# A hybrid encoder layer in split fp32: operand combinations dealt out between gated-unit tiles, mixed tiles loaded into the scan's copy pages, and two casts of the feed-forward asked for one piece later

## The chip, the core and the metric

The kernel runs on one core of a Trainium2 chip. The time is the device time of one execution in microseconds (us); the time of a kernel is the median of its runs. Engines are named as the profile does: PE is TensorE (PEld its weight loads), DVE VectorE, ACT ScalarE, POOL GpSimd, SP SyncE, whose queue issues nearly all DMAs.

## What is computed

One encoder layer over x of 1024 positions and 1024 channels, all in float32:

```
h    = rmsnorm(x)
proj = h @ w_in                                  # 1024 x 8192, cut into 8 parts
glu_in, q, v, z_f, z_b, og, g_a, g_b = split(proj)
a    = glu(glu_in)                               # 512 channels
a    = silu(layernorm(dwconv31(a))) @ conv_pw_w  # mixer A
o    = hgrn2 scan over q, v, z_f + the same backwards over z_b   # 8 heads of 128
b    = (rmsnorm per head(o) * silu(og)) @ hgrn_o_w               # mixer B
x    = x + (sigmoid(g_a) * a + sigmoid(g_b) * b) @ w_out
h2   = rmsnorm(x)
gate, val = split(h2 @ ffn_w_up)
x    = x + (silu(dwconv3(gate)) * val) @ ffn_w_down
out  = rmsnorm(x)
```

## The kernel before

**Products in split fp32.** A float32 operand is kept as two tiles, a rounded part and a rest: `split` (L124) makes the first with a cast on ScalarE and the second with a subtraction on VectorE. A product of two such operands is three matmuls (L148 to L150) into one PSUM bank. Weights come as `wr` pages (512 KB, two of them) through SyncE's queue (L135) and are split into `wp` pages; activations lie in `hx` and `hy` pages of 128 x 512.

**Seven products for eight.** Most of the large products use Strassen's scheme: seven products of half-size blocks, each with a sum or difference of blocks on either side. The activations' sums are made by `combos` (L457 on): it takes three blocks `b11`, `b12`, `b22`, makes b12 - b22 into a `tm` page, and from that two further blocks in place, each split at once (rows L465 and L124 with `hy`). The function `h_combos` (L936 on) does this for the four values of k: it loads three blocks from the DRAM copy `d_h` into `su` pages (four of them) and calls `combos`. The weights' sums are made by a generator (around L414) that hands control back with `yield n`: its next step comes n pieces of matmul later.

**Streams.** Matmul work is cut into pieces. A `Stream` holds generators of such pieces, and `fill(n)` writes n of them into the program where it is called, so that TensorE's work stands between the other engines' work. The order of the text is then the order in which the pieces are handed to a scheduler at build time, which orders each engine's queue; an instruction waits for its operands and for its page to come free, and every queue is in order.

**The first place, 75 to 125 us.** The gated unit's tiles (`s_glu`) are projections whose banks are read by a sigmoid on ScalarE (L850) and a multiplication on VectorE (L856). They are followed by the 31-tap convolution on VectorE (L1035, L1038, into `acc`), which runs through the whole convolution stage beside the pair jobs on TensorE up to about 345 us; the pair jobs' banks are read by VectorE at L799. Before, all four calls of `combos` are handed over first and then 17 pieces of the gated unit:

```
    h_combos()
    s_glu.fill(GLU_LATE)
```

**The second place, 825 to 905 us.** The scan over 16 half-heads alternates with dense work. It copies `qF` and `kG` into `A` pages (L1175, eight of them), turns `kG` on TensorE (L1320) and copies it to `kT` (L1322), for the state products of L1329. Each head's mixed output (`bm`) goes to DRAM, but for the last head. Behind the scan, `bm_loads` brings the seven others back, half by half, for the product with `hgrn_o_w` (mixer B): `load` (L117) takes one of four `tm` pages, and the tile is split into `hx` pages.

Of the kernel before, what the change touches and what calls it, by code (L numbers as in the profile page):

```python
# [29 lines left out]
GLU_LATE = 17  # L30
# [17 lines left out]
def tile_hybrid_encoder(  # L48
# [22 lines left out]
    nc = tc.nc  # L71
    PSUM = bass.MemoryType.PSUM
    V, A, G, T = nc.vector, nc.scalar, nc.gpsimd, nc.tensor
# [20 lines left out]
    def nm(s):  # L94
        uid[0] += 1
        return f"{s}_{uid[0]}"
# [6 lines left out]
    def page(pool, tag, bufs, dt=F32):  # L103
        return pool.tile([P, H], dt, tag=tag, name=nm(tag), bufs=bufs)

    def tmp():
        return page(mp, "tm", 4)
# [4 lines left out]
    def hx():  # L112
        return page(mp, "hx", 32, F32R)

    def load(src):
        t = tmp()
        nc.sync.dma_start(t, src)  # L117
        return t
# [4 lines left out]
    def split(hi, lo, src, eng, late=False):  # L123
        parts = A.copy(hi, src), eng.tensor_tensor(lo, src, hi.bitcast(F32), op=ALU.subtract)  # L124
        if late:
            for i in parts:
                pin(i)
        return hi, lo
# [9 lines left out]
    def w_page(nk, pool=None):  # L138
        if pool is None:
            return mp.tile([P, nk, P], F32R, tag="wp", name=nm("wp"), bufs=4)  # L140
        return pool.tile([P, nk, P], F32R, tag="wq", name=nm("wq"), bufs=3)
# [140 lines left out]
    def pair_job(src0, src1, nk, acts, wpool, pool, evac, su=4, first=False, late=False, now=False, direct=False, columns=1, take=None, stored=None):  # L282
# [7 lines left out]
        def steps(w):  # L290
            def both(src, alt, late=late):
                hi, lo = split(w_page(2 * nk, alt), w_page(2 * nk, alt), src, V, late)
                return [(hi[:, :nk], lo[:, :nk]), (hi[:, nk:], lo[:, nk:])]

            def add(o, a):
                if first:
                    V.tensor_tensor(o, o, a, op=ALU.add)
                elif direct:
                    pin(V.tensor_tensor(o, o, a, op=ALU.add))
                else:  # L300
                    G.dma_start(o, a, accum_op=ALU.add)

            if take is not None:

                def raw(src=None, n=2 * nk):
                    t = wpool.tile([P, n, P], F32, tag="sr", name=nm("sr"), bufs=4)
                    if src is not None:
                        nc.sync.dma_start(t, src)
                    return t

                def plus(o, a, b):
                    pin(V.tensor_tensor(o, a, b, op=ALU.add))

                rows = raw(src0)
                if stored is None:
                    other = raw(src1)
                    yield 4
                    w[1], w[2] = both(rows, None)
                    col, sums, a22 = raw(), rows, other[:, nk:]
                    plus(col[:, :nk], rows[:, :nk], other[:, :nk])  # L320
                    plus(col[:, nk:], other[:, :nk], other[:, nk:])
                    yield 2
                    plus(rows[:, :nk], rows[:, :nk], col[:, nk:])
                    plus(rows[:, nk:], rows[:, nk:], rows[:, :nk])
                    yield 4
                else:
                    yield 2
                    col = raw(stored[0])
                    yield 2
                    w[1], w[2] = both(rows, None)  # L330
                    sums = raw(stored[1])
                    yield 3
                    a22 = raw(src1[:, nk:], nk)
                    yield 3
                w[7], w[5] = both(col, pool)
                yield 3
                w[6], w[3] = both(sums, None)
                yield 3
                one = w_page(2 * nk, pool)
                w[4] = split(one[:, :nk], one[:, nk:], a22, V, late)  # L340
                return

            def column_page():
                return wpool.tile([P, 2 * nk, P], F32, tag="sw", name=nm("sw"), bufs=columns)

            def quadrant():
                a22 = pool.tile([P, nk, P], F32, tag="w4", name=nm("w4"), bufs=1)
                nc.sync.dma_start(a22, src1[:, nk:])
                return a22

            rows = raw_w(src0, 2 * nk)
            if stored is not None:
                sums = raw_w(stored[1], 2 * nk)
                col = column_page()
                nc.sync.dma_start(col, stored[0])
                yield 0 if now else 4
                w[1], w[2] = both(rows, None, not now)
                if now:
                    yield 0
                    w[6], w[3] = both(sums, None, False)  # L360
                    yield 1
                a22 = quadrant()
                yield 2 if now else 6
                w[7], w[5] = both(col, pool)
                if not now:
                    yield 3
                    w[6], w[3] = both(sums, None)
                yield 3
                one = w_page(2 * nk, pool)
                w[4] = split(one[:, :nk], one[:, nk:], a22, V, late)  # L370
                return

            col = column_page()
            nc.sync.dma_start(col[:, :nk], src0[:, :nk])
            nc.sync.dma_start(col[:, nk:], src1[:, :nk])
            if first:
                other = column_page()
                nc.sync.dma_start(other, src1)
                add(col, other)
            elif not direct:  # L380
                add(col, src1)
            def sums():
                add(rows[:, :nk], col[:, nk:])
                add(rows[:, nk:], rows[:, :nk])

            if now:
                w[1], w[2] = both(rows, None, False)
                sums()
                yield 0
                w[6], w[3] = both(rows, None, False)  # L390
                yield 1
                a22 = quadrant()
                yield 2
                w[7], w[5] = both(col, pool)
                yield 4
            elif direct:
                yield 2
                other = raw_w(src1, 2 * nk)
                yield 2
                w[1], w[2] = both(rows, None)  # L400
                a22 = quadrant()
                yield 6
                add(col, other)
                sums()
                yield 1
                w[6], w[3] = both(rows, None)
                yield 1
                w[7], w[5] = both(col, pool)
                yield 4
            else:  # L410
                yield 4
                w[1], w[2] = both(rows, None)
                sums()
                a22 = quadrant()  # L414
                yield 6
                w[7], w[5] = both(col, pool)
                yield 3
                w[6], w[3] = both(rows, None)
                yield 3
            one = w_page(2 * nk, pool)  # L420
            w[4] = split(one[:, :nk], one[:, nk:], a22, V, late)

# [37 lines left out]
    def combos(ops, k, b11, b12, b22, alloc):  # L460

        def sub(o, a, b):
            V.tensor_tensor(o, a, b, op=ALU.subtract)  # L465

        def parts(i, src):
            ops[i].append(split(alloc(), alloc(), src, V))

        t3 = page(mp, "tm", 4)  # L470
        sub(t3, b12, b22)
        parts(7, t3)
        sub(b22, t3, b11)
        parts(6, b22)
        sub(b12, b11, b12)
        parts(5, b12)
# [88 lines left out]
    d_bm = scratch("d_bm", NH, 2)  # L565
# [19 lines left out]
    NK2 = ND // 2  # L585
# [350 lines left out]
    def h_combos():  # L936
        def hy():
            return page(p1, "hy", 24, F32R)

        for k in range(NK2):  # L940
            b11, b12, b22 = (page(p1, "su", 4) for _ in range(3))
            for t, (kk, half) in ((b11, (k, 0)), (b12, (k, 1)), (b22, (k + NK2, 1))):
                nc.sync.dma_start(t, d_h[kk][half])
            combos(ht, k, b11, b12, b22, hy)

    s_glu = Stream(run_jobs(glu_jobs(), prime=1, first=GLU_LEAD))
    s_glu.fill()
# [14 lines left out]
    s_glu.fill(GLU_MORE)  # L962
    p0.release()
    p1 = tc.alloc_tile_pool(name="p1", bufs=1, reuse_waits="tile")
    h_combos()
    s_glu.fill(GLU_LATE)
    pair0 = in_pair(0)
    w_pair0 = pair0[0]()
    s_glu.drain()
# [162 lines left out]
    for k in range(NK2):  # L1132
        t = load(d_h[k][1])
# [4 lines left out]
    hp = tc.alloc_tile_pool(name="heads", bufs=1, reuse_waits="tile")  # L1138
# [294 lines left out]
    bm = [[None, None] for _ in range(NH)]  # L1433

    def bm_loads(half):
        for h in range(NH - 1):
            bm[h][half] = split(hx(), hx(), load(d_bm[h][half]), V)

    NI = 2 * NH
    cur = Base(scan_inputs(0))  # L1440
# [600 lines left out]
```

## Time and profile before

| | |
|---|---|
| median of 3 runs | 1730.4 us (1727.42 to 1732.26) |
| the profiled execution | 1733.97 us, its span 1732.2 us |
| TensorE's granted clock, mean | 0.996 |
| busy share of the span | TensorE 98%, VectorE 72%, ScalarE 48%, GpSimd 12% |
| DMA | 308 MB, 178 GB/s |

A row such as `99.14 0.69 DVE L465 TENSOR_TENSOR ... [1.69 <-DMA su<-d_h]` gives the start in the span, the duration, the engine, the line and the operation; the bracket is the idle time of the engine just before and what ended it. Rows that follow each other without a bracket follow without idle time; a next row's start can lie ahead of the end of the one before, since instructions overlap in their pipeline. "SPq" rows are the issues of DMAs on SyncE's queue, with "x2" for several in a row. In the table of stretches the granted clock is 1.00 at full speed.

### The profile page before, as it was taken

How to read it: one execution, taken by the hardware profiler on the slowest of the kernel's cores; microseconds unless marked ns; L12 is line 12 of the kernel's file. 1: busy time of each engine (PE TensorE's matmuls, PEld its weight loads, DVE VectorE, ACT ScalarE, POOL GpSimd, SP SyncE). 2: the span in 40 equal slices, each digit the busy share in tenths (PEclk: the TensorE clock that was granted, in tenths of full speed). 3: DMA queues.
4: the chain of work that ended last, by engine and by line, in shares of the span. 5: the costliest groups of instructions: out<-in, count | busy, mean ns of one | idle time of the engine just before them, and what ended most of it. 6: DMA issues, size and time to landing. Idle time of an engine off the chain costs nothing. (4 is left out here: it accounts for less than half of the span.)

```text
span 1732.2 us, 30782 instructions
## 1 busy us (share of the span) xinstructions
PE 1704.5 (98%) x11902; PEld 1416.5 (82%) x11902; DVE 1255.2 (72%) x1937; ACT 826.1 (48%) x1544; POOL 206.5 (12%) x249
## 2 busy tenths in 40 slices
PE   8999999999999999999999999999999999999998
PEld 6878888788788888888878888888888788888787
DVE  4599999746778888888566466666767776657864
ACT  7444443334566777776442245444334443542334
POOL 2211111100001111111100002011111111000110
PEclk9999999999999999999999999999999999999999
DMA  8778888854673434436579466567777777783842
GB/s 287 236 173 183 192 194 192 199 165 151 207 238 101 134 126 132 127 114 211 185 258 318 143 206 196 146 149 160 158 168 168 161 179 162 226 263 105 215 93 98
DMA packets 336585, 308.29 MB, mean 178 GB/s; under 512 B 17070, under 2 KB 248630, under 8 KB 336438
## 3 DMA queue, kind: packets, MB, share of 16 engines
q1 hardware_dynamic: 289590, 267.51, 48.9%
q0 software_dynamic: 46848, 38.81, 15.3%
q8 instruction: 93, 1.52, 0.4%
q14 instruction: 54, 0.44, 0.1%
HBM read 201.40 MB, written 87.03 MB: 167 GB/s over the span
## 5 line engine op out<-in xcount | busy, mean ns | idle before, releaser
L148 PE MATMUL mm<-hx,wp 128*128 128x512 f32 x1068 | 429.0, 402 | 5.9 <-ACT tm L850 2.5
L150 PE MATMUL mm<-hx,wp 128*128 128x512 f32 x1068 | 418.4, 392 | 1.0 <-DVE wp L124 0.9
L149 PE MATMUL mm<-hx,wp 128*128 128x512 f32 x1068 | 417.8, 391 | 0.5 <-DVE hx L124 0.5
L124 ACT CAST wp<-wr 128x1024 fp32r<-128x1024 f32 (+2 forms) x147 | 147.4, 1004 | 270.6 <-DMA wr<-wr 115.3
L148 PEld LDWEIGHTS mm<-hx,wp 128*128 128x128 f32 x1068 | 201.3, 188 | 50.8 <-ACT su L439 3.2
L150 PEld LDWEIGHTS mm<-hx,wp 128*128 128x128 f32 x1068 | 201.2, 188 | 47.2 <-DVE wp L124 4.4
L149 PEld LDWEIGHTS mm<-hx,wp 128*128 128x128 f32 x1068 | 201.6, 189 | 40.7 <-DVE hx L124 1.4
L124 DVE TENSOR_TENSOR wp<-wr,wp 128x1024 fp32r<-128x1024 f32 (+2 forms) x145 | 169.5, 1170 | 82.0 <-ACT wp L124 79.1
L1038 DVE SCALAR_TENSOR_TENSOR acc<-gl,v_b,acc 128x1024 f32<-128x1024 f32 x120 | 149.0, 1278 | 0.4
L439 ACT COPY su<-mm 128x512 f32<-128x512 f32 x82 | 47.7, 581 | 58.8 <-PE mm L150 58.7
L148 PE MATMUL tr<-hx,wp 128*128 128x512 f32 x180 | 70.5, 392 | 0.0
L150 PE MATMUL tr<-hx,wp 128*128 128x512 f32 x180 | 70.0, 389 | 0.0
L149 PE MATMUL tr<-hx,wp 128*128 128x512 f32 x180 | 70.0, 389 | 0.0
L1310 POOL DMA_DIRECT2D S<-D x64 | 35.5, 560 | 286.7 <-ACT jk L1375 127.7
L1143 DVE TENSOR_TENSOR qF<-qF,tb 128x512 f32<-128x512 f32 x96 | 65.5, 686 | 4.6 <-ACT A L1175 4.6
L1637 DVE SCALAR_TENSOR_TENSOR tm<-gp,v_a,tm 128x512 f32<-128x512 f32 x88 | 66.0, 750 | 3.8 <-ACT tm L1635 2.0
L124 ACT CAST wq<-sw 128x1024 fp32r<-128x1024 f32 x41 | 43.2, 1054 | 52.3 <-PE mm L149 43.0
L1143 DVE TENSOR_TENSOR kG<-kG,tb 128x512 f32<-128x512 f32 x96 | 65.2, 686 | 0.3
L148 PE MATMUL mm<-hy,wp 128*128 128x512 f32 x164 | 64.2, 391 | 0.0
L148 PE MATMUL sc<-hy,wq 128*128 128x512 f32 x164 | 64.2, 391 | 0.0
L150 PE MATMUL sc<-hy,wq 128*128 128x512 f32 x164 | 63.8, 389 | 0.0
L149 PE MATMUL mm<-hy,wp 128*128 128x512 f32 x164 | 63.8, 389 | 0.0
(373 smaller groups left out, 3679.4 us busy)
## 6 DMA issues: line engine op xcount, KB each, us to landing
wr<-in_w_in_dram SPq DMA_DIRECT2D x48, 512.0 KB, 4.3
wr<-in_ffn_w_up_dram SPq DMA_DIRECT2D x22, 512.0 KB, 6.2
sw<-in_w_in_dram SPq DMA_DIRECT2D x38, 256.0 KB
d_g<-ft SPq DMA_DIRECT2D x38, 256.0 KB, 3.4
sw<-in_ffn_w_up_dram SPq DMA_DIRECT2D x38, 256.0 KB, 4.1
sw<-in_ffn_w_up_dram POOLq DMA_DIRECT2D x19, 512.0 KB, 7.9
wr<-sw POOLq DMA_DIRECT2D x32, 256.0 KB, 3.8
wr<-wr POOLq DMA_DIRECT2D x32, 256.0 KB, 4.3
```

What stands on the lines that cost most here:

```text
L124: parts = A.copy(hi, src), eng.tensor_tensor(lo, src, hi.bitcast(F32), op=ALU.subtract)
L148: T.matmul(acc, whi[:, k, :], ahi, start=first, stop=False, skip_group_check=again)
L149: T.matmul(acc, whi[:, k, :], alo, start=False, stop=False, skip_group_check=again)
L150: T.matmul(acc, wlo[:, k, :], ahi, start=False, stop=last, skip_group_check=again)
L439: A.copy(t, acc)
L1038: V.scalar_tensor_tensor(acc, g[:, k : k + S], tap(k), acc, op0=ALU.mult, op1=ALU.add)
L1143: V.tensor_tensor(o, a, b, op=op)
L1310: G.dma_start(S_t[g : g + 32, :, g : g + 32], D_t[g : g + 32])
L1637: V.scalar_tensor_tensor(c, g[:, o + k : o + k + H], vec("fdw", k * NF + j), c, op0=ALU.mult, op1=ALU.add,)
```

## The change

Three edits. `h_combos` becomes a generator that yields behind each of its four calls of `combos`, and after each of them 4 of the 17 pieces of the gated unit are written, the last one behind the loop. `bm_loads` takes an `A` page of the scan's pool in place of a `tm` page. And in the weights' generator of the pair jobs (its last branch) the sixth and third sums are made 4 pieces after the ones before them, not 3, and the fourth 2 pieces after those, not 3.

```diff
@@ pair job's weights @@
                 w[7], w[5] = both(col, pool)
-                yield 3
+                yield 4
                 w[6], w[3] = both(rows, None)
-                yield 3
+                yield 2
             one = w_page(2 * nk, pool)
...
@@ h_combos @@
             combos(ht, k, b11, b12, b22, hy)
+            yield
...
     p1 = tc.alloc_tile_pool(name="p1", bufs=1, reuse_waits="tile")
-    h_combos()
-    s_glu.fill(GLU_LATE)
+    for _ in h_combos():
+        s_glu.fill(GLU_LATE // NK2)
+    s_glu.fill(GLU_LATE % NK2)
     pair0 = in_pair(0)
...
     def bm_loads(half):
         for h in range(NH - 1):
-            bm[h][half] = split(hx(), hx(), load(d_bm[h][half]), V)
+            t = page(hp, "A", 8)
+            nc.sync.dma_start(t, d_bm[h][half])
+            bm[h][half] = split(hx(), hx(), t, V)
```

Behind the edit of `h_combos` all line numbers are 1 or 2 higher, so L1035 and L1038 become L1037 and L1040, L1322 becomes L1324, and so on. TensorE's order is the same in both kernels, and so is GpSimd's; the weights' edit moves no row on any engine by itself.

SyncE's queue at the first place, before. The `su` rows are the operands of combinations, `wr` the weights of gated-unit tiles, `w_262` a block of a pair job's weights:

```order
L135 DMA wr_1315<-in_w_in_dram 128x8x128
L943 DMA su_1206<-d_h_1_101 128x512
L943 DMA su_1207<-d_h_1_109 128x512
L135 DMA wr_1348<-in_w_in_dram 128x8x128
L943 DMA su_1227<-d_h_0_102 128x512
L348 DMA w_262_1577<-in_w_in_dram 128x4x128
L943 DMA su_1228<-d_h_1_103 128x512
L943 DMA su_1229<-d_h_1_111 128x512
L135 DMA wr_1380<-in_w_in_dram 128x8x128
```

The same place in the changed kernel:

```order
L135 DMA wr_1293<-in_w_in_dram 128x8x128
L943 DMA su_1271<-d_h_1_101 128x512
L135 DMA wr_1348<-in_w_in_dram 128x8x128
L943 DMA su_1272<-d_h_1_109 128x512
L943 DMA su_1324<-d_h_0_102 128x512
L348 DMA w_262_1577<-in_w_in_dram 128x4x128
L135 DMA wr_1380<-in_w_in_dram 128x8x128
L943 DMA su_1325<-d_h_1_103 128x512
L943 DMA su_1326<-d_h_1_111 128x512
```

The third operand of the third combination (the load of `d_h_1_109`) now stands behind the weight load `wr_1348`, and the last two of the fourth behind `wr_1380`, where each stood ahead of it.

VectorE's queue at this place, before:

```order
L1035 TENSOR_SCALAR acc_1532<-gl_473,v_b,v_a 128x1024
L465 TENSOR_TENSOR tm_1211<-su_1206,su_1207 128x512
L1038 SCALAR_TENSOR_TENSOR acc_1532<-gl_473,v_b,acc_1532 128x1024
L465 TENSOR_TENSOR su_1207<-tm_1211,su_1205 128x512
L124 TENSOR_TENSOR hy_1214<-tm_1211,hy_1213 128x512
L465 TENSOR_TENSOR su_1206<-su_1205,su_1206 128x512
L124 TENSOR_TENSOR hy_1219<-su_1207,hy_1218 128x512
L124 TENSOR_TENSOR wp_1318<-wr_1315,wp_1317 128x1024
L124 TENSOR_TENSOR hy_1224<-su_1206,hy_1223 128x512
L1038 SCALAR_TENSOR_TENSOR acc_1532<-gl_473,v_b,acc_1532 128x1024
L465 TENSOR_TENSOR tm_1233<-su_1228,su_1229 128x512
L856 TENSOR_TENSOR gl_464<-mm_1289,tm_1281 128x512
```

In the changed kernel, from the same convolution row on:

```order
L1037 TENSOR_SCALAR acc_1532<-gl_473,v_b,v_a 128x1024
L1040 SCALAR_TENSOR_TENSOR acc_1532<-gl_473,v_b,acc_1532 128x1024
L856 TENSOR_TENSOR gl_464<-mm_1245,tm_1237 128x512
L465 TENSOR_TENSOR tm_1276<-su_1271,su_1272 128x512
L124 TENSOR_TENSOR wp_1296<-wr_1293,wp_1295 128x1024
L124 TENSOR_TENSOR hy_1279<-tm_1276,hy_1278 128x512
L465 TENSOR_TENSOR su_1272<-tm_1276,su_1270 128x512
L465 TENSOR_TENSOR su_1271<-su_1270,su_1271 128x512
L1040 SCALAR_TENSOR_TENSOR acc_1532<-gl_473,v_b,acc_1532 128x1024
L124 TENSOR_TENSOR hy_1284<-su_1272,hy_1283 128x512
L124 TENSOR_TENSOR wp_1351<-wr_1348,wp_1350 128x1024
L124 TENSOR_TENSOR hy_1289<-su_1271,hy_1288 128x512
```

The gated unit's multiplication (L856) stands ahead of the third combination now, and the weight subtraction `wp_1296` (the one that was `wp_1318`) right behind its first operation. On ScalarE the sigmoid of that multiplication, which stood behind the cast of the weight `wr_1348`, stands behind a cast of the second combination.

ScalarE's queue at the second place, in the changed kernel. `A_10103` is the scan's last copy of that half, the `hx` rows cast the loaded mixed tiles of heads 0 to 5, `kT` are the turned keys and `ob` the scan's output bank:

```order
L1177 COPY A_10103<-qF_9770 128x2x16x16
L124 CAST hx_10574<-A_10572 128x512
L124 CAST hx_10580<-A_10578 128x512
L124 CAST hx_10586<-A_10584 128x512
L1374 COPY tm_10079<-ob_10067 128x512
L1324 COPY kT_10110<-tr_10105 128x512
L1377 ACTIVATE jk_10081,oss_9929<-tm_10079 128x128
L1324 COPY kT_10117<-mm_10112 128x512
L1377 ACTIVATE jk_10083,oss_9929<-tm_10079 128x128
L124 CAST hx_10592<-A_10590 128x512
```

Before, no `hx` row stood here: the copy of `ob` followed `A_10103` at once, and the seven casts of this half stood some 40 rows later.

## The prediction

> **What bounds the kernel now.** I read the page's busy times first, then the waits of TensorE, then the stretches around each wait, with their granted clock.
>
> ```profile
> PE 1704.5 (98%) x11902; PEld 1416.5 (82%) x11902; DVE 1255.2 (72%) x1937; ACT 826.1 (48%) x1544; POOL 206.5 (12%) x249
> ```
>
> TensorE is busy for 98% of the span and the change takes no matmul away, so there is little to win: only TensorE's waits, and the time at half clock. Of the waits these two concern the change (total us, times, longest), others follow as rows:
>
> ```profile
> PE mm L148 <- ACT tm L850: 2.5, 1, 2.5
> PE mm L149 <- DVE hx L124: 0.5, 2, 0.2
> ```
>
> The stretches show what a wait costs besides its own length. The columns are the stretch, its length, then busy time of PE, PEld, DVE, ACT and POOL, then the granted clock, DMA share and GB/s:
>
> ```profile
> 94.14:97.56 3.42, 1.26 (x6) 0.72 (x4) 3.31 (x4) 1.69 (x3) 0.00 (x0) 1.00 1.06 338
> 97.56:100.97 3.41, 3.08 (x7) 2.48 (x8) 1.83 (x4) 1.39 (x3) 0.15 (x1) 0.50 0.82 248
> ...
> 899.69:903.10 3.41, 2.18 (x8) 1.17 (x8) 2.49 (x4) 1.14 (x2) 0.00 (x0) 1.00 1.05 316
> 903.10:906.52 3.42, 3.42 (x10) 2.68 (x9) 3.07 (x5) 1.57 (x2) 0.00 (x0) 0.50 1.08 370
> 120.00:300.00 180.00, 180.00 (x796) 149.05 (x795) 178.55 (x186) 73.01 (x102) 31.66 (x29) 1.00 0.83 188
> ```
>
> TensorE idles 2.2 us in the first stretch (3.42 less 1.26) and the next one runs at 0.50; it idles 1.2 us in the third and the fourth runs at 0.50. A halved stretch of 3.41 us does the work of 1.7, so each costs 1.7 us more. The last row decides the first place: over the 180 us of the convolution stage VectorE is busy 178.55 and TensorE all of it. Both are full, so time that TensorE alone gains just before it is not kept, unless VectorE gains it too.
>
> **First place: combinations dealt out among the gated-unit tiles (75 to 125 us).** The rows are of ScalarE, TensorE, SyncE's queue, GpSimd and VectorE:
>
> ```profile
> 96.30 1.05 ACT L124 CAST wp<-wr 128x1024 fp32r<-128x1024 f32 x1 [1.73 <-DMA wr<-in_w_in_dram]
> 97.25 1.08 ACT L850 ACTIVATE tm<-mm 128x512 f32<-128x512 f32 x2
> 97.89 0.80 PE L148 MATMUL mm<-hx,wp 128*128 128x512 f32 x1 [2.49 <-ACT tm L850]
> 88.18 0.38 SPq L135 DMA_DIRECT2D wr<-in_w_in_dram  x1
> 93.94 0.92 SPq L943 DMA_DIRECT2D su<-d_h  x2
> 86.28 1.76 POOL L301 DMA_DIRECT2D sw<-in_w_in_dram  x1 [21.31 <-DMA sw<-in_w_in_dram]
> 81.64 0.69 DVE L465 TENSOR_TENSOR tm<-su,su 128x512 f32<-128x512 f32 x1
> 82.25 1.22 DVE L124 TENSOR_TENSOR wp<-wr,wp 128x1024 fp32r<-128x1024 f32 x1
> 83.39 0.69 DVE L124 TENSOR_TENSOR hy<-tm,hy 128x512 fp32r<-128x512 f32 x1
> 89.27 0.81 DVE L1035 TENSOR_SCALAR acc<-gl,v_b,v_a 128x1024 f32<-128x1024 f32 x1
> 90.22 0.69 DVE L465 TENSOR_TENSOR tm<-su,su 128x512 f32<-128x512 f32 x1
> 90.83 1.28 DVE L1038 SCALAR_TENSOR_TENSOR acc<-gl,v_b,acc 128x1024 f32<-128x1024 f32 x1
> 92.02 0.69 DVE L465 TENSOR_TENSOR su<-tm,su 128x512 f32<-128x512 f32 x1
> 99.14 0.69 DVE L465 TENSOR_TENSOR tm<-su,su 128x512 f32<-128x512 f32 x1 [1.69 <-DMA su<-d_h]
> ```
>
> What it removes: the sigmoid at L850 stands behind a weight cast that waits for a load until 96.30, and TensorE waits 2.49 us for the PSUM bank. In the new order L850 stands right behind a cast of the second combination, near 87 us, so this wait goes.
>
> What it adds: on SyncE the third operand of a combination now stands behind the 512 KB weight load that it led before, and VectorE's in-order queue waits for it. From row to row VectorE takes 0.60 us for a 512-wide operation, 1.14 for a 1024-wide subtraction, 0.95 for L1035 and 1.2 for L1038. In the new order, between 81.64 and the waiting combination, stand three of 1.14, eight of 0.60, one of 0.95 and one of 1.2: 81.64 + 3.42 + 4.80 + 0.95 + 1.2 = 92.0. The weight load goes out near 87.6 (its page is released by the third of these subtractions, at 87.5), the operand near 88.2. Before, the weight load issued at 88.18 was only there at 96.30, with GpSimd's adding load of 86.28 beside it. So I estimate the operand's landing at 95.8: the same 8.1 us from the weight's earlier issue (95.7) and 0.1 for the operand behind it. The low bound is no wait (92.0, the operand overtakes), the high one is 96.3 plus 256 KB at the 338 GB/s of the first stretch, 0.8: 97.1.
>
> From the landing it takes 0.60 + 1.14 + 4 x 0.60 + 1.2 = 5.34 us until VectorE has done what it had done before at 99.14: 101.1, so it is 2.0 later (-1.8 to +3.3). A second wait follows: the next combination's third operand can be asked for only then, at 101.2, and is wanted 1.14 + 0.60 + 1.2 = 2.9 us later. Before, such a load of 93.94 to 94.86 landed by 99.14, at least 4.3 us after its issue, with other loads ahead; with an empty queue it can be in time. So 0 to 1.6; I take 0.5, nearer to no wait since the weight load ahead of it has 3.6 us of lead.
>
> The convolution stage passes the lag on. At its end stand:
>
> ```profile
> 304.26 0.50 PE L148 MATMUL mm<-hx,wp 128*128 128x512 f32 x1 [0.62 <-DVE ev L799]
> 321.82 1.23 DVE L124 TENSOR_TENSOR wq<-sw,wq 128x1024 fp32r<-128x1024 f32 x1 [0.24 <-ACT wq L124]
> 327.62 1.22 DVE L124 TENSOR_TENSOR wp<-wr,wp 128x1024 fp32r<-128x1024 f32 x1 [0.38 <-ACT wp L124]
> 340.80 1.42 DVE L1052 TENSOR_TENSOR tm<-tm,cx 128x512 f32<-128x512 f32 x2 [6.52 <-DMA cx<-d_cv]
> ```
>
> TensorE already waits there for VectorE's evacuation, so a later VectorE is a later TensorE; VectorE has slack again only at 340. Its two waits for ScalarE (0.24 and 0.38) absorb 0.6. First place: 2.0 + 0.5 - 0.6 = **+1.9 us** (-1.8 to +4.9). TensorE's own gain of 2.49 plus a halved stretch does not count, for the reason above; it will also wait some 1.8 us at 95.9 for a weight subtraction that now stands behind the combination (done at 95.8 + 0.60 + 1.14 = 97.5), in place of the wait that went.
>
> **Second place: mixed tiles loaded into the scan's copy pages (825 to 905 us).** The rows are of SyncE's queue, ScalarE and TensorE, first at the new place of the loads, then at the old one:
>
> ```profile
> 828.13 0.32 SPq L1104 DMA_DIRECT2D ev<-d_ga  x1
> 833.53 0.59 ACT L1322 COPY kT<-tr 128x512 f32<-128x512 f32 x1
> 834.31 0.59 ACT L1322 COPY kT<-mm 128x512 f32<-128x512 f32 x1
> 835.09 1.05 PE L1329 MATMUL sc<-v,kT 128*128 128x128 f32 x8
> 888.39 1.80 SPq L117 DMA_DIRECT2D tm<-d_bm  x4
> 894.35 1.64 SPq L117 DMA_DIRECT2D tm<-d_bm  x3
> 892.98 2.62 ACT L124 CAST hx<-tm 128x512 fp32r<-128x512 f32 x4 [5.00 <-DMA tm<-d_bm]
> 896.99 1.29 ACT L124 CAST hx<-tm 128x512 fp32r<-128x512 f32 x2 [1.39 <-DMA tm<-d_bm]
> 899.92 0.62 ACT L124 CAST hx<-tm 128x512 fp32r<-128x512 f32 x1 [1.65 <-DMA tm<-d_bm]
> 883.90 0.47 PE L148 MATMUL mm<-hx,wp 128*128 128x512 f32 x1 [0.36 <-DVE ev L1105]
> 884.94 0.50 PE L150 MATMUL mm<-hx,wp 128*128 128x512 f32 x1 [0.34 <-DVE wp L124]
> 900.59 0.50 PE L148 MATMUL mm<-hx,wp 128*128 128x512 f32 x1 [0.77 <-ACT hx L124]
> ```
>
> Before, the loads go through four "tm" pages, so they go out as pages come free (888.39, 894.35), and the last casts wait for them. With pages of their own they are asked for ahead of that; TensorE's waits for them go: 0.77, the two at L149 (0.5 in the list of waits) and, as I choose, the 0.36 and 0.34 at 884, whose loads and casts stand behind such loads and casts; in all 1.9. With the 1.2 us idle gone the halved stretch at 903 goes too, 1.7: -3.6.
>
> The cost is at 833. Six of the first seven loads move up to right behind 828.13, and three of their casts now stand on ScalarE ahead of the two kT copies, for which TensorE waits at 835.09. Issued from 828.5 to 829.7, three loads are there at 831 at the earliest; with the 3.6 to 4.6 us that I take for one in such company (4.3 as in the row of 93.94) the third lands near 833.7, its cast of 0.5 and two copies of 0.5 end at 835.4 to 836.1. So +0.4, between 0 and 1.0, and a halved stretch of 1.7 if this trips the clock. Second place: **-3.2 us** (-3.6 to -0.9).
>
> **Third place, the feed-forward's casts:** nothing. The generator hands over one piece later, but on every engine the rows around these casts stand in the same order as before. Were they moved, their cover is matmuls, of which TensorE has enough.
>
> **Sum:** 1.9 - 3.2 + 0 = -1.3 us (-5.4 to +4.0). The profiled execution took 1733.97 us with a span of 1732.2; from it comes 1732.7. The median of the runs is 3.6 lower, 1730.4; from it **1729.1 us**.
>
> **A rule on the clock.** The rows put half clock behind 2.2 and 1.2 us of idle time within a stretch. The Trainium skill ("TensorE: Matmul & The Clock Gate", "Part 1: The HAM clock gate (the "warmup" mystery)") says that the gate halves after at least one idle window of about 3.4 us; the trace disagrees, since 1.2 us was enough. By that rule the second place's idle would not be why its stretch is halved, and the 1.7 would stay.
>
> **The rivals.**
> *Operands in time.* The third operand lands before the weight load that it stands behind, or both early. Then VectorE's 1.69 at 99.14 goes and nothing takes its place: -1.8, and the second place gives its full -3.6: -5.4, 1725.0. For it: two loads at 88 us have 4 us until 92.0. Against: 8.1 us for the weight load before. Chance 0.22.
> *Late loads halve the clock.* The operands land at the high bounds (+4.9). Then the lag reaches TensorE as one wait of over 1.2 us, at an evacuation such as 304.26, and halves the next stretch (+1.7); the copies at 833 do the same (-0.9 for the second place). +5.7, 1736.1. It decides from 1.2 us of idle time in one stretch, and the forecast's lag of 1.9 is above that, if it comes in one piece. Against: the lag may come in pieces, as TensorE has waits for ScalarE and VectorE at several places. Chance 0.26.
> *The halved stretch at 903 stays*, for a reason other than the idle time: -1.3 + 1.7 = +0.4, 1730.8. Chance 0.06.
>
> **How the numbers follow.** The forecast keeps 0.46. About 0.3% (5.2 us) is what a measurement of this kernel can tell from no change. The first rival is beyond it (faster 0.22), the second too (slower 0.26), the rest is within it (0.52). The range takes in both outer cases, with half a microsecond for the scatter of the runs: 1724.5 to 1736.5.
>
> **What would show it.** Right: no wait of TensorE for L850; a wait of VectorE for su near 92 to 96; no wait for d_bm casts after 880 and full clock at 903; a wait for kT under 1 us at 835. Wrong: VectorE without a wait in 90 to 105, or new stretches at 0.50 in 140 to 345.

## The result and the profile after

| | before | changed |
|---|---|---|
| median of 14 runs each | 1730.39 us (1727.19 to 1732.69) | 1732.88 us (1730.81 to 1737.22) |
| ratio to before | | 1.0020, 95% interval 1.0012 to 1.0028 |
| profiled execution, its span | 1733.97, 1732.2 us | 1732.56, 1730.5 us |

The changed kernel is 0.2% slower, 2 to 5 us; the forecast was 1.3 us faster. The two profiled executions alone would say the opposite, since the one of before lies 3.6 us above its median and the changed one at its own. So the reading goes by stages. TensorE runs the same matmuls in the same order in both, so the start of the matmul with the same number can be compared. In the changed kernel's profile TensorE is 0.7 us ahead at the beginning of the convolution stage, 4.8 us behind at its end (345 us), 6.1 behind at 835, and only 1.8 behind at 908. The second place gained what was forecast and the first lost much more than that.

TensorE's waits in the changed kernel, in the order of their sums (total us, times, longest):

```profile
PE mm L148 <- DVE ev L799: 4.6, 6, 1.6
...
PE mm L150 <- DVE wp L124: 3.6, 4, 1.6
...
PE sc L1331 <- ACT kT L1324: 1.0, 1, 1.0
```

The waits for the sigmoid and for the mixed tiles' casts are gone from the list. In their place stand six waits for VectorE's evacuations (0.6 us before), four for its weight subtractions (0.9 before) and one for the kT copy.

The first place, changed kernel: VectorE's rows, the two waits of TensorE, and the stretches that correspond to those shown of before:

```profile
90.50 0.68 DVE L856 TENSOR_TENSOR gl<-mm,tm 128x512 f32<-128x512 f32 x1
95.51 0.69 DVE L465 TENSOR_TENSOR tm<-su,su 128x512 f32<-128x512 f32 x1 [4.32 <-DMA su<-d_h]
103.79 0.68 DVE L465 TENSOR_TENSOR tm<-su,su 128x512 f32<-128x512 f32 x1
97.39 0.50 PE L150 MATMUL mm<-hx,wp 128*128 128x512 f32 x1 [1.56 <-DVE wp L124]
109.86 0.50 PE L150 MATMUL mm<-hx,wp 128*128 128x512 f32 x1 [1.30 <-DVE wp L124]
94.14:97.55 3.41, 1.85 (x9) 1.23 (x8) 2.04 (x3) 0.62 (x1) 0.00 (x0) 1.00 0.76 173
97.55:100.97 3.42, 3.42 (x16) 2.80 (x17) 3.42 (x6) 2.40 (x4) 0.16 (x1) 1.00 0.59 167
```

The operand came at 95.5 (forecast 95.8); VectorE waited 4.32 us for it. The second wait, for the fourth combination, did not come (103.79 has no bracket). TensorE's 1.56 us of idle time left the next stretch at full clock.

The convolution stage, changed kernel:

```profile
171.85 0.50 PE L148 MATMUL mm<-hx,wp 128*128 128x512 f32 x1 [1.25 <-DVE ev L799]
245.10 0.81 DVE L1037 TENSOR_SCALAR acc<-gl,v_b,v_a 128x1024 f32<-128x1024 f32 x1 [2.08 <-DMA d_cv<-acc]
305.70 0.69 DVE L1052 TENSOR_TENSOR tm<-cx 128x512 f32<-128x512 f32 x1 [1.36 <-DMA cx<-d_cv]
306.31 0.68 DVE L799 TENSOR_TENSOR ev<-su,mm 128x512 f32<-128x512 f32 x1
307.04 0.50 PE L148 MATMUL mm<-hx,wp 128*128 128x512 f32 x1 [0.65 <-DVE ev L799]
328.01 0.50 PE L148 MATMUL mm<-hx,wp 128*128 128x512 f32 x1 [1.61 <-DVE ev L799]
345.60 1.42 DVE L1054 TENSOR_TENSOR tm<-tm,cx 128x512 f32<-128x512 f32 x2 [6.94 <-DMA cx<-d_cv]
```

Two waits of VectorE come up on the way: 2.08 us for a page of the accumulator whose store is not done, and 1.36 us for a reloaded tile (cx), with an evacuation right behind it in the queue. TensorE pays at the evacuations.

The wait at 171.85 has another cause, which shows in the order of VectorE's rows. Dealing out changed that order through the whole stage, far behind the place that was edited. The first three rows are of before, the others of the changed kernel, with ScalarE's cast first:

```profile
168.10 0.68 DVE L799 TENSOR_TENSOR ev<-su,mm 128x512 f32<-128x512 f32 x1
168.70 1.22 DVE L124 TENSOR_TENSOR wq<-sw,wq 128x1024 fp32r<-128x1024 f32 x1
169.83 1.28 DVE L1038 SCALAR_TENSOR_TENSOR acc<-gl,v_b,acc 128x1024 f32<-128x1024 f32 x1

167.69 1.05 ACT L124 CAST wq<-sw 128x1024 fp32r<-128x1024 f32 x1 [1.91 <-PE mm L149]
168.78 1.23 DVE L124 TENSOR_TENSOR wq<-sw,wq 128x1024 fp32r<-128x1024 f32 x1 [0.36 <-ACT wq L124]
169.92 1.28 DVE L1040 SCALAR_TENSOR_TENSOR acc<-gl,v_b,acc 128x1024 f32<-128x1024 f32 x1
171.12 0.68 DVE L799 TENSOR_TENSOR ev<-su,mm 128x512 f32<-128x512 f32 x1
```

The evacuation (L799) stood ahead of a weight subtraction and a tap of the convolution, and now stands behind them. The subtraction waits 0.36 us for ScalarE's cast, which itself waited for TensorE, so the wait closes a loop between the three engines.

The second place, changed kernel: ScalarE, TensorE, and two stretches:

```profile
837.50 0.62 ACT L124 CAST hx<-A 128x512 fp32r<-128x512 f32 x1 [2.85 <-DMA A<-d_bm]
839.56 0.62 ACT L124 CAST hx<-A 128x512 fp32r<-128x512 f32 x1 [0.51 <-DMA A<-d_bm]
840.56 0.59 ACT L1324 COPY kT<-tr 128x512 f32<-128x512 f32 x1
841.20 1.16 PE L1331 MATMUL sc<-v,kT 128*128 128x128 f32 x8 [1.01 <-ACT kT L1324]
841.59:845.00 3.41, 3.41 (x24) 3.06 (x24) 2.00 (x5) 2.87 (x10) 0.99 (x2) 1.00 0.57 198
903.02:906.43 3.41, 3.41 (x17) 2.83 (x16) 3.10 (x6) 0.00 (x0) 0.00 (x0) 1.00 1.03 368
```

ScalarE waits for the loads, the kT copies come 1.01 us late, and the stretch near 903 runs at full clock.

### The profile page after: what moved, and what is told of

It is laid out like the page before. It is cut to its first block, busy times and chain, and to the rows that moved or that the text cites. A ratio compares the mean times of both kernels' runs of the same rounds, so it can differ in the third digit from the quotient of the medians.

```text
span 1730.5 us, 30753 instructions
## 1 busy us (share of the span) xinstructions
PE 1700.3 (98%) x11902; PEld 1414.0 (82%) x11902; DVE 1257.0 (73%) x1937; ACT 824.3 (48%) x1544; POOL 206.5 (12%) x249
## 4 chain that ended last, share of the span: by engine, by line
PE 55%; DMA 2%; DVE 1%; issue 0%; ACT 0%; POOLq 0%; ACTq 0%; DVEq 0%
PE mm L148 13%; PE mm L150 13%; PE mm L149 13%; PE sc L148 3%; PE sc L150 3%; PE sc L149 3%; PE tr L148 1%; PE tr L150 1%; PE tr L149 1%; PE ob L1372 1%; DMA d_a<-ev 1%; PE sc L1331 0%; PE sc L1196 0%; PE mm L1331 0%; PE sc L1282 0%
## 5 line engine op out<-in xcount | busy, mean ns | idle before, releaser
L1040 DVE SCALAR_TENSOR_TENSOR acc<-gl,v_b,acc 128x1024 f32<-128x1024 f32 x120 | 148.9, 1276 | 0.5
L439 ACT COPY su<-mm 128x512 f32<-128x512 f32 x82 | 47.7, 582 | 73.3 <-PE mm L150 73.0
```

Source lines behind the costliest of these rows:

```text
L439: A.copy(t, acc)
L1040: V.scalar_tensor_tensor(acc, g[:, k : k + S], tap(k), acc, op0=ALU.mult, op1=ALU.add)
```

## The experiments

Times are ratios to before in runs on the same chip, with the 95% interval. The stage table counts, for one profiled execution of each, how much longer than in the first profile of before (us) TensorE took to the 1500th matmul (about 345 us), from there to the 7700th (about 830), from there to the 8215th (about 908) and from there to the end:

| kernel | to 345 | to 830 | to 908 | rest |
|---|---|---|---|---|
| changed | +4.8 | +0.1 | -3.2 | -3.5 |
| e1 dealing only | +4.4 | +2.1 | -1.8 | +0.4 |
| e2 pages only | -1.4 | +0.6 | -3.1 | +2.0 |
| e3 changed, third operand apart | +6.5 | +0.2 | -4.2 | +2.2 |
| e4 pages, third operand apart | +3.5 | +2.1 | -2.7 | +0.9 |
| e5 changed, operands by GpSimd | +10.7 | +0.1 | -2.9 | -1.0 |
| e6 changed, cx sum held | +3.4 | +1.8 | -2.7 | -0.3 |
| e7 pages, cx sum held | -2.7 | -0.1 | -3.5 | +0.1 |
| e8 before again | -2.3 | +1.5 | -0.8 | -2.7 |
| e9 dealing, cx sum held | +2.2 | 0.0 | -1.5 | +1.7 |
| e10 pages, casts and cx sum held | -2.6 | +2.0 | -4.4 | -3.3 |

In the second column, the entries from +1.5 to +2.1 (e1, e4, e6, e8, e10) hold one halved stretch each, between 588 and 599 us; the other executions have none there.

**e1, e2: each edit alone.** Before with the edit of `h_combos` and its loop (e1), and with that of `bm_loads` (e2). The weights' edit was not run alone: it moves no row.

> Only the dealing out of the combinations, the rest as before. Theory 1 (VectorE's lag): VectorE waits over 4 us for the third combination's operand behind a weight load, and the lag that this leaves grows to about 5 us over the convolution stage: 5 us slower than before (1735.5), with the wait near 91 to 96 us and TensorE waiting at L799 several times between 120 and 345 us. Rival (the mixed tiles' loads are the cost): dealing out costs the 1.9 us of the forecast or less (1732.3), and the second place has lost its gain.

Measured: 1736.27 us, ratio 1.0029 (1.0017 to 1.0041), +5 us. TensorE waits for VectorE at L799 as in the changed kernel:

```profile
PE mm L148 <- DVE ev L799: 4.3, 5, 1.6
```

> Only the mixed tiles' loads in the scan's copy pages, the rest as before. Theory 1: the second place gains what the traces show between 830 and 910 us, about 3.3 us (1727.1): a wait of about 1 us for kT near 836, none for the mixed tiles' casts near 900, full clock there. Rival (the mixed tiles' loads are the cost): 0.6 us slower or no change (1730.4 to 1731.0).

Measured: 1730.28 us, ratio 1.0001 (0.9986 to 1.0015). The stage at 830 to 908 us gained 3.1 us, with a wait of 1.27 us for kT, but the whole time did not show it: its 12 runs spread from 1726.28 to 1738.97, and in its profile the feed-forward gave 3.7 us back between 1145 and 1190 us, at waits for an evacuation on ScalarE (L439). So dealing out is the cost. The time is that of the rival, the gain in the stage that of theory 1; what the pages bring in the whole time is not settled by this run.

**e3, e4: the operand's wait taken away.** The third operand of each combination in one of the evacuation pages (`ev`), with both edits (e3) and with the pages alone (e4):

```diff
-            b11, b12, b22 = (page(p1, "su", 4) for _ in range(3))
+            b11, b12, b22 = page(p1, "su", 4), page(p1, "su", 4), ev()
```

> The changed kernel with the third operand of each combination in an evacuation page, so that four pages serve two operands each and the loads no longer wait for the combination before. Theory 1: VectorE's wait of 4.3 us for the third combination goes, VectorE enters the convolution stage about 2.6 us ahead of the kernel before, and this much or more is kept to 345 us; with the second place's 3.3 it gives 6 us faster than before (1724.4), 8 us faster than the changed kernel. Rival (the lag comes from the new order of VectorE's rows in the convolution stage, not from the wait): TensorE still waits at L799 and the time stays at 1731 to 1733.

Measured: 1739.08 us, ratio 1.0043 (1.0031 to 1.0055). The 4.3 us wait did go, and TensorE was 4.6 us ahead of before at 101 us. At 172 us it was 1.4 us behind, after waits of 2.04 us (130 us, with a halved stretch behind it) and of 1.25 us for evacuations. VectorE's waits from 60 to 350 us in e3, the few of them that differ:

```profile
DVE tm L1052 <- DMA cx<-d_cv: 3.7, 1, 3.7
...
DVE acc L1037 <- DMA d_cv<-acc: 2.5, 1, 2.5
...
DVE ev L799 <- issue: 2.2, 1, 2.2
DVE su L977 <- DMA su<-d_h: 1.8, 1, 1.8
```

> The mixed tiles' loads in the copy pages and the third operand in an evacuation page, without dealing out. Theory 1: VectorE's 1.7 us wait of before near 98 us goes, so 1.7 faster than the loads' change alone: 5.0 us faster than before (1725.4). Rival (TensorE sets the end of this stage, through its wait for the sigmoid at L850 of 2.5 us and the halved stretch): the time is that of the loads' change alone, since TensorE's wait for L850 stays.

Measured: 1738.09 us, ratio 1.0036 (1.0021 to 1.0051), with waits of VectorE for cx of 3.0 and for the accumulator of 2.5 us, and TensorE waiting 4.4 us at L799. Both kernels also got another order of taps and evacuations, so they don't isolate the wait. They refute the simple theory that whoever brings VectorE into the stage earlier keeps it.

What they do show is the rival of e3's expectation, the order of the rows. In all seven kernels with the subtraction ahead of the evacuation (changed, e1, e3, e4, e5, e6, e9) TensorE waits 1.25 us at this evacuation, whether it had come there 2.7 us ahead of before (e4) or 3.2 us behind (e5); in the five with the old order (before, e2, e7, e8, e10) it does not wait there. VectorE was no later in e4 than in the kernels of the old order at its seventh tap (2.3 us ahead of before, they at most 1.6), and at the last tap it was 2.3 us behind before. So in the new order the stage makes a lag even where VectorE comes early.

Both kernels then have a long wait for an evacuation behind the cx sum, and a halved stretch after it (3.0 us at 309 in e3; the rows are of e4):

```profile
306.21 0.50 PE L148 MATMUL mm<-hx,wp 128*128 128x512 f32 x1 [2.31 <-DVE ev L799]
303.44:306.86 3.42, 1.11 (x6) 0.60 (x5) 3.19 (x4) 0.62 (x1) 0.00 (x0) 1.00 0.26 46
306.86:310.27 3.41, 3.41 (x10) 2.64 (x9) 3.41 (x5) 0.00 (x0) 0.00 (x0) 0.50 0.71 225
```

**e5: the operands through another queue.** `nc.gpsimd.dma_start` in place of `nc.sync.dma_start` in `h_combos`.

> The changed kernel, with the combinations' operands loaded through GpSimd's queue in place of SyncE's, so that no operand stands behind a weight load; VectorE's order in the convolution stage stays but for single swaps. Theory 1 (the wait for the operand is what VectorE carries through the stage): the 4.3 us wait at 95 us goes or shrinks below 1 us, and TensorE's lag at 345 us, 4.8 us in the changed kernel, falls by 3 to 4: 1729 us. Theory 2 (the lag is made by the stage's own waits, for the accumulator's page near 245 us and for cx near 305 us, which are set by DMAs): VectorE comes early and waits longer there, the lag at 345 us stays over 3 us: 1732 to 1733.

Measured: 1740.45 us, ratio 1.0038 (1.0025 to 1.0051). It did not take the wait away, so it decides nothing between the theories as they stood. VectorE and GpSimd's queue:

```profile
95.05 0.69 DVE L465 TENSOR_TENSOR tm<-su,su 128x512 f32<-128x512 f32 x1 [3.30 <-DMA su<-d_h]
88.20 0.55 POOL L943 DMA_DIRECT2D su<-d_h  x1 [1.16 <-DVE hy L124]
```

The operand no longer stood behind the weight load and was there at 95.05 all the same, 6.9 us after its issue. But on GpSimd's queue it stood behind the adding load, issued at 82.60 and landed 10.8 us later (93.4). So the run does not separate the place in a queue from the traffic of that time: shown is that the other queue brought the operand 0.5 us earlier and no more. The lag at 345 us, 10.7, holds a wait of VectorE for cx of 4.6 us and two halved stretches (98 and 313 us).

**e6, e7, e9: the sum over the reloaded tiles held.** The first sum over cx is pinned to its place in the program, behind the pieces ahead of it, so it no longer stands ahead of evacuations:

```diff
-    def total(ts, o):
-        V.tensor_tensor(o, ts[0], ts[1], op=ALU.add)
+    def total(ts, o, hold=False):
+        first = V.tensor_tensor(o, ts[0], ts[1], op=ALU.add)
+        if hold:
+            pin(first)
...
-        T.matmul(mean, ones_m, total(xs, tmp()), start=True, stop=True)
+        T.matmul(mean, ones_m, total(xs, tmp(), half == 0), start=True, stop=True)
```

> The changed kernel with the first sum over the convolution's reloaded tiles held in program order, so that it stands behind the taps and evacuations. Theory 2: VectorE's wait of 1.4 us for cx near 305 us no longer stands ahead of an evacuation, TensorE's waits at 307 and 328 us shrink, the lag at 345 us falls from 4.8 to about 3.4: 1731.4. Theory 1 alone (only the operand's wait of 4.3 us counts): the lag at 345 us stays at 4.5 to 5, 1732.9.

Measured: 1734.9 us, ratio 1.0013 (1.0001 to 1.0025). The lag at 345 us was 3.4, but this execution had a half-clock stretch at 99 us that the changed kernel's had not, and entered the stage 1.7 us later. From 130 us to 345 us TensorE lost 2.5 us on the first profile of before, the changed kernel 5.4.

> The mixed tiles' loads in the copy pages with the sum held behind the evacuations, without dealing out. Both theories: no wait for cx stood ahead of an evacuation here but the one of 6.4 us near 340, which cost TensorE nothing up to then: within 1 us of the loads' change alone, TensorE's lag at 345 us between -2 and 0; the gain of 3 us between 830 and 910 us is there again. If the wait near 340 was on the path after all, 1 to 2 us faster than that.

Measured: 1731.34 us, ratio 0.9995 (0.9983 to 1.0007); to 345 us 1.3 us less than e2. The lag there, -2.7, lies outside the expected -2 to 0; 0.8 of the 1.3 us is there at 121 us already.

> Only the dealing out, with the sum over the reloaded tiles held behind the evacuations. Theory 2 (the lag is the sum of VectorE's waits: for the operand at 95 us, for the accumulator's page at 245, for cx at 305): as with both changes, holding the sum takes 2.5 to 3 us off the stage from 130 to 345 us, so the dealing out alone costs 2 us in place of 5: 1733.5. Theory 1 alone: the stage stays 5 us longer than before, 1736.3.

Measured: 1734.08 us, ratio 1.0017 (1.0003 to 1.0031), between the two expectations' 1733.5 and 1736.3 and nearer to the first. To 345 us it took 2.2 us less than e1; from 130 us on it lost 2.7 us, e1 5.1. TensorE's waits at L799 in e9:

```profile
PE mm L148 <- DVE ev L799: 2.8, 3, 1.3
```

The wait of 1.6 us at 328 us, which the changed kernel and e1 have, is gone in e6 and e9. So the cx sum's place ahead of evacuations is part of the lag (some 2.2 us with dealing out, about 0.8 without, by e7 and e10 against e2 and e8), and not all of it.

**e8: before again.** No edit.

> The kernel before, once more, for a second profile of it. The stages to 910 us should agree with the first profile within 0.5 us. The feed-forward stage behind 1145 us differed by 3 to 4 us between the profiles of kernels that are alike there; if that is the scatter of single executions, the two profiles of before differ there as well.

Measured: one run, 1729.9 us. The stages did not agree within 0.5 us, and between 1145 and 1190 us the two executions of before differed by 0.4 us only, from 908 us to the end by 2.7. This execution had no half-clock stretch at 97 us, and its wait for L850 was 1.50 us. At 885 us it waited longer than the first and was halved there, not at 903. The first rows are TensorE's, then three stretches:

```profile
96.51 0.50 PE L148 MATMUL mm<-hx,wp 128*128 128x512 f32 x1 [1.50 <-ACT tm L850]
884.66 0.47 PE L148 MATMUL mm<-hx,wp 128*128 128x512 f32 x1 [1.80 <-ACT hx L124]
97.55:100.97 3.42, 3.42 (x16) 2.81 (x15) 3.27 (x6) 1.39 (x3) 0.67 (x5) 1.00 0.56 183
882.83:886.25 3.42, 1.29 (x5) 0.76 (x5) 3.12 (x5) 3.19 (x5) 0.00 (x0) 0.96 0.48 168
886.25:889.66 3.41, 3.41 (x10) 2.66 (x9) 3.41 (x5) 1.14 (x2) 0.00 (x0) 0.54 0.84 260
```

**e10: the first half's casts of the mixed tiles held too.** On e7:

```diff
-            bm[h][half] = split(hx(), hx(), t, V)
+            bm[h][half] = split(hx(), hx(), t, V, half == 0)
```

> The mixed tiles' loads in the copy pages, the first half's casts of them held behind the scan's copies, and the sum held, without dealing out. If the three casts ahead of the kT copies are what costs 1.3 us between 830 and 883 us, that goes and the whole second place gains 4 us; 1 us faster than without holding: 1729 to 1730, and full clock at 903. If the casts, now later on ScalarE, come late for the product with hgrn_o_w, TensorE waits there (near 905 us) and 2 to 3 us of the gain is lost.

Measured: 1730.15 us, ratio 0.9988 (0.9973 to 1.0003). From 830 to 908 us it gained 4.4, the wait for kT went, and this is all that TensorE waits for from 825 to 910 us:

```profile
PE mm L150 <- DVE wp L124: 0.3, 1, 0.3
```

It is the best of the versions that were run, and its gain over before, 2 us, is within what its runs can tell from none.

## Why the prediction was wrong

**The step that failed: "First place: +1.9 us", and in it "The convolution stage passes the lag on".** Dealing out alone measured +5.0 us (1.0029 of 1731.3; 2.9 to 7.1 by the interval). The sum took VectorE's waits in the stage from the rows of before, as if only the rows near 90 us changed places; what the runs show in their place is a new order through the whole stage, which adds waits of its own.

- *The operand's landing* came out as forecast, 95.5 against 95.8, and VectorE was at the point that it had reached at 99.14 by 100.9 (forecast 101.1). That is in part luck: the weight load went out 0.8 us earlier than reckoned and landed 7.5 us after its issue, not 8.1, at 94.3; the operand came 1.2 us behind it, not 0.1. Whether the weight load ahead in the queue made it late stays open (e5).
- *The base was wrong.* The 2.0 us were counted from one execution of before, and that one was late at just this place. In e2, e7, e8 and e10, where this part is as before, VectorE's convolution is 0.6 to 1.6 us earlier at its seventh L1038 row than in that execution, which had waited 0.61 us for another load at 80 us. In the changed kernel, e1 and e9 it is 1.4 to 1.9 us later. The entry lag is therefore 2.9 us between the means of the two groups, not 2.0.
- *"Its two waits for ScalarE absorb 0.6"* was wrong in sign. By the starts of the four accumulations, the lag between the same two groups is 2.9 at the second, 3.8 at the third, 4.8 at the fourth, and 5.7 us at the last tap (without held sums). The two waits, 0.24 and 0.38 us at 322 and 328 in before, are one of 0.28 in the changed kernel, and two new ones for ScalarE's weight casts (0.36 and 0.35 us, at 169 and 189) add 0.7; 0.2 to 0.8 us is the longer wait for the accumulator's page (1.5 to 2.1 us against 1.3), and 1.4 to 1.5 the new wait for cx. Some half a microsecond is not assigned. That each adds just its length is argued from the rows. Shown is that dealing out makes the lag, that with the cx sum held the stage costs 2.2 us less (e9), and that TensorE's 1.25 us at 171 come from the order of the rows. What a late operand alone would cost in the old order is not shown: no run has that.
- *The second wait* (0.5) did not come.

**"TensorE's own gain ... does not count"** held in the changed kernel: 0.7 us ahead at 121 us, it waited for VectorE by 151. The new wait for the weight subtraction was 1.56 us; the prediction's own terms (97.5 less 95.9) give 1.6, not its 1.8. In e8, without the halved stretch, TensorE was 2.5 us ahead at 302 us and kept it, with VectorE ahead as well. But VectorE's lead of 1.2 us was there at 88 us, ahead of that stretch, so it does not show that the stretch had held VectorE back.

**"Second place: -3.2 us"** came out at -3.2 in the changed kernel and -3.1 in e2 against the first profile of before; the kT wait was 1.0 where 0.4 was taken, at the high bound, and did not halve a stretch. Against the four profiles without the pages (0, -0.8, -1.5, -1.8) it is about 2 us, since the halved stretch that the sum counted as certain was there in two of the four (the two of before) and not in e1 and e9.

**"Third place: nothing"** stands, by the order alone.

**The sum**, with what the runs show: 5 for the first place and -2 for the second, +3 us; measured +2.5 by the medians and +3.5 by the ratio. Of the rivals, operands in time did not come (a wait of 4.32 us), and the halved stretch at 903 went. The late loads' price (1736.1) was too high and their mechanism half there: the changed kernel waited 1.61 us at an evacuation, but no stretch was halved. In e3, e4 and e5, with waits of 2.3 to 4.0 us at an evacuation between 306 and 314 us, the next stretch was halved, as that rival had it.

**The rule on the clock.** I had put half clock behind 1.2 us of idle time. The changed kernel had 1.56 us of idle time in the stretch at 95 us and 1.01 at 839, both followed by full clock; its 1.61 us at 328 fell into two stretches, 1.06 us in the first. Before had half clock behind 1.2. So a single row does not give a threshold. By the clock records the halved stretches of one execution start whole multiples of 3.413 us apart (97.55 and 903.10 in before are 236 of them). Counted in stretches laid out so, between 60 and 1700 us of all twelve profiles, 13 of the 14 halved ones follow a stretch with 1.8 us or more of idle time, and no stretch with more than 1.9 is followed by full clock (e9 had 1.86 and full clock). The one exception is that at 903 us in before, behind 1.2 us; why it was halved is not shown. The Trainium skill ("TensorE: Matmul & The Clock Gate", "Part 1: The HAM clock gate (the "warmup" mystery)") speaks of a free-running window; the runs here agree by these multiples, and disagree with a whole idle window being needed.

## What to carry to other kernels

Where two engines are both full through a stage, find the one whose queue the stage's end hangs on, and compare its whole order before and after through the stage, not only near the edit. Then follow a delay along that new order to every wait that it will meet: here stores whose pages came free late, casts, and reloads that the order put ahead of an evacuation added to the delay. Take the base of a sum of a few microseconds from more than one execution, and count a halved stretch by the share of executions that show it. Moving a late load to another queue helps little where it stands behind another long load there: here it brought 0.5 us.

## What was not expected of the hardware

- An operand of 256 KB took 6.9 us (GpSimd's queue) to 8.1 us (SyncE's, issued at 87.4) with a weight load and an adding load in flight.
- Idle times of TensorE of 1.01 and 1.56 us within a stretch left the next one at full clock, where 1.2 and 2.2 us in before halved it; a halved stretch came or stayed away between two executions of one kernel.
- In the feed-forward, between 1145 and 1190 us, executions of kernels that are alike there differed by up to 4.9 us (-1.2 to +3.7 against the first profile of before), with TensorE waiting for ScalarE's evacuation (L439).
